# One split instruction per engine over a whole weight chunk, in a two-block transformer kernel

## The chip, the cores and the metric

The kernel runs on one core of one Trainium2 chip. The metric is the device time in microseconds (us) of one execution; the time before is the median of three runs. Five engines take part: TensorE (PE, with its weight loads shown apart as PEld), VectorE (DVE), ScalarE (ACT), GpSimd (POOL) and SyncE (SP), which here only issues DMAs. Each engine works off its own instructions strictly in the order in which the program gives them, and waits on semaphores of the others.

## What is computed

Two transformer stacks run one after the other over 256 tokens of width 1024, each two layers deep, all in float32. Every layer is a mixer and a gated feed-forward network, each behind an RMS norm. Cut to the parts that matter here:

```python
for l in range(2):                       # first block
    h = rms_norm(x, norm1_g[l]); proj = h @ w_in[l]          # 1024 x 3584
    ret = chunk_retention(...); sb = stick_breaking(...)     # 4 heads each
    x = x + concat([ret, sb]) @ w_out[l]
    h = rms_norm(x, norm2_g[l])
    x = x + (silu(h @ w_gate[l]) * (h @ w_up[l])) @ w_down[l]   # D_FF 2816
for l in range(2):                       # second block
    h = rms_norm(x, g_mix[l]); proj = h @ w_in_2[l]
    merged = sum over 3 branches of gate * (branch @ w_p)    # latent, dilated and neighbourhood attention
    x = x + merged @ w_o[l]
    h = rms_norm(x, g_ffn[l])
    x = x + (silu(h @ w1[l]) * (h @ w3[l])) @ w2[l]
return rms_norm(x, g_final)
```

## The kernel before

All weights lie in one array in memory, cut on the host into 502 chunks in the order of their use. A chunk is 128 partitions by 1024 columns of float32 (512 KB); 32 of them have 768 columns. Each chunk is loaded by one DMA into a tile `raw` (4 buffers), and is then split into a pair `hi`, `lo` (6 buffers each): ScalarE writes `hi`, the value rounded to the matmul's type, and VectorE writes `lo = raw - hi`. The products are made of three terms, `hi*hi`, `hi*lo` and `lo*hi`: `mm3` (lines 264 to 266) as three matmuls, `mmw` as two, one of 512 columns for `hi` against both parts of the activations (line 324) and one of 256 columns for `lo` (line 325).

The user of a chunk calls `chunk()`, which first asks for the splits of the next four chunks and for the loads of three more, and then hands out its own pair. So a chunk is normally split five uses ahead. A buffer of `hi` or `lo` comes free when the last matmul on it has run.

The split of a chunk is done today in pieces of `CUT = 512` columns: `hi` of the first half, `lo` of the first half, `hi` of the second half, `lo` of the second half. A matmul waits only for the pieces that it reads.

The order of the instructions on each engine is not written out by hand. A scheduler walks through a modelled execution, and gives each engine, when it is free in that model, the ready instruction of the highest priority. Priority is the order in which the program text asks for things, except in a block marked `high_priority` (`URGENT`), which is put ahead: the sums into the residual `x` and the norm that follows (`add`, lines 527 and 528, `norm_pair`, lines 452 and 453). An instruction that has begun isn't interrupted. On the chip the order is then fixed, and the times are not those of the model.

What else runs on ScalarE and VectorE, and so stands in the same two queues: `second` (line 366) copies one half of a product out of the accumulator bank, `whole` (line 371) adds the other half to it, both before the bank can be used again; in the attention parts `softmax_bank` (lines 850 to 861), `p_T` (line 867, the copy `pT` of transposed probabilities) and `finish`; at the start of a layer part the norm's `rsqrt` (line 402 on VectorE, then a power on GpSimd, line 403) and `row_bcast` (line 557, `diag`), which feeds two small matmuls.

At the end of `mixer2`, and at the beginning of each feed-forward network, `wide4` uses four chunks at once, column tile by column tile, and ends all four at nearly the same time.

Of the kernel before, what the change touches and what calls it, by code (L numbers as in the profile page):

```python
# [201 lines left out]
class Net:  # L202
# [16 lines left out]


    RAW, HI, LO = 4, 6, 6
    CUT = 512

    def fetch(self, upto):
        nc = self.nc
# [9 lines left out]
    def split(self, upto):  # L235
        nc = self.nc
        while self.next_split < min(upto, len(self.sizes)):
# [5 lines left out]
            lo = self.wp.tile([128, CW], F32R, tag="lo", bufs=self.LO, name="lo")  # L243
            for c in range(0, n, self.CUT):
                c = slice(c, min(n, c + self.CUT))
                nc.scalar.copy(out=hi[:, c], in_=raw[:, c])  # L246
# [889 lines left out]
```

## Time and profile before

| | |
|---|---|
| median of 3 runs | 1593.51 us (1593.07 to 1596.3) |
| the profiled execution | 1597.04 us, its span 1595.3 us |
| granted TensorE clock, mean over the span | 0.996 |
| busy: PE, PEld, DVE, ACT, POOL | 98%, 85%, 69%, 55%, 7% |
| memory read | 266.78 MB |

The span goes from the first to the last instruction; the 1.74 us by which the execution is longer lie around it. Busy times are unions of the instructions' records. Matmuls are pipelined and their ends are modelled, so PE's 98% says that it seldom stood still, and not that it was at its peak.

### The profile page before, as it was taken

Reading aid. Unit: us, or ns where it says so; the run is one execution under the profiler, and the core shown is the slowest. Engines: PE = TensorE matmul, PEld = TensorE weight load, DVE = VectorE, ACT = ScalarE, POOL = GpSimd, SP = SyncE. Lnnn points to the kernel's source line nnn. Section 1 sums busy time; section 2 is a strip of 40 time slices with the busy share of each in tenths; the row PEclk is TensorE's granted clock in tenths of the full one; section 3 lists DMA queues with packets and bytes.
Section 4 is the critical chain, followed back from the end, with each engine's and each line's share of the span. In section 5 each row is a group of like instructions: output and inputs, shape, how many; then the busy total and the mean of one; then the engine's idle time right before and its main releaser. Section 6 shows DMA issues by size and latency. Waiting matters only on the chain.

```text
span 1595.3 us, 23916 instructions
## 1 busy us (share of the span) xinstructions
PE 1568.5 (98%) x8908; PEld 1353.4 (85%) x8908; DVE 1106.1 (69%) x1957; ACT 872.5 (55%) x1687; POOL 117.8 (7%) x117
## 2 busy tenths in 40 slices
PE   9999999999999999999999999999999999999997
PEld 6888888888988888898888888888898888888886
DVE  7876777767777767775656677766775656677763
ACT  6555655555555555455544565555455544565552
POOL 2001000100110003100001110001000001110001
PEclk9999999999999999999999999999999999999998
DMA  7554655654455566533544465556433544465561
GB/s 255 178 157 161 202 190 183 193 176 140 158 175 196 180 187 230 177 106 106 185 139 159 136 207 185 181 181 223 161 107 109 186 136 159 143 200 189 178 185 55
DMA packets 78629, 269.39 MB, mean 169 GB/s; under 512 B 8625, under 2 KB 12849, under 8 KB 78385
## 3 DMA queue, kind: packets, MB, share of 16 engines
q1 hardware_dynamic: 78224, 267.34, 51.5%
q8 instruction: 70, 1.15, 0.3%
q10 hardware_dynamic: 288, 0.52, 0.1%
q14 instruction: 47, 0.38, 0.1%
HBM read 266.78 MB, written 1.05 MB: 168 GB/s over the span
## 4 chain that ended last, share of the span: by engine, by line
PE 94%; DVE 3%; issue 1%; ACT 1%; POOL 1%; DMA 0%; DVEq 0%; ACTq 0%
PE mm L324 36%; PE mm L325 18%; PE mm L266 9%; PE mm L265 9%; PE mm L264 9%; PE sc L269 4%; PE ov L269 3%; PE pt L416 2%; DVE lo L247 1%; PE pt L269 1%; ACT hi L246 1%; PE sc L265 0%; PE sc L266 0%; PE sc L264 0%; DVE xT L453 0%
## 5 line engine op out<-in xcount | busy, mean ns | idle before, releaser
L247 DVE TENSOR_TENSOR lo<-raw,hi 128x512 fp32r<-128x512 f32 x1004 | 669.8, 695 | 358.1 <-ACT hi L246 354.9
L246 ACT CAST hi<-raw 128x512 fp32r<-128x512 f32 x1004 | 581.3, 613 | 540.2 <-PE mm L324 204.5
L324 PE MATMUL mm<-xT,hi 128*128 128x512 f32 x1664 | 585.0, 396 | 5.2 <-DVE t L371 3.4
L325 PE MATMUL mm<-xT,lo 128*128 128x256 f32 x1664 | 466.6, 281 | 0.0
L324 PEld LDWEIGHTS mm<-xT,hi 128*128 128x128 f32 x1664 | 312.1, 188 | 79.2 <-DVE t L371 3.7
L325 PEld LDWEIGHTS mm<-xT,lo 128*128 128x128 f32 x1664 | 314.4, 189 | 0.3
L324 PE MATMUL mm<-hT,hi 128*128 128x512 f32 x704 | 246.6, 395 | 0.6 <-DVE t L371 0.6
L265 PE MATMUL mm<-lo,xT 128*128 128x512 f32 (+1 forms) x544 | 213.8, 393 | 1.7 <-DVE lo L247 1.7
L264 PE MATMUL mm<-hi,xT 128*128 128x512 f32 (+1 forms) x544 | 213.2, 392 | 1.1 <-ACT hi L246 1.1
L266 PE MATMUL mm<-hi,xT 128*128 128x512 f32 (+1 forms) x544 | 213.5, 392 | 0.0
L325 PE MATMUL mm<-hT,lo 128*128 128x256 f32 x704 | 197.4, 280 | 0.0
L324 PEld LDWEIGHTS mm<-hT,hi 128*128 128x128 f32 x704 | 131.9, 187 | 31.4 <-DVE t L371 0.7
L325 PEld LDWEIGHTS mm<-hT,lo 128*128 128x128 f32 x704 | 133.0, 189 | 0.0
L265 PEld LDWEIGHTS mm<-lo,xT 128*128 128x128 f32 x544 | 102.8, 189 | 21.3 <-DVE lo L247 2.9
L264 PEld LDWEIGHTS mm<-hi,xT 128*128 128x128 f32 x544 | 102.8, 189 | 20.0 <-ACT hi L246 1.6
L266 PEld LDWEIGHTS mm<-hi,xT 128*128 128x128 f32 x544 | 102.8, 189 | 18.1
L366 ACT COPY part<-mm 128x512 f32<-128x512 f32 x129 | 74.6, 578 | 10.1 <-PE mm L325 10.1
L472 POOL TENSOR_TENSOR acc<-acc,sq 128x256 f32<-128x256 f32 x58 | 60.9, 1053 | 169.0 <-ACT sq L463 166.3
L469 POOL TENSOR_TENSOR acc<-sq 128x256 f32<-128x256 f32 x10 | 15.0, 1507 | 690.7 <-ACT sq L463 690.7
L867 DVE COPY pT<-pt 128x512 f32<-128x512 f32 x48 | 33.1, 691 | 26.2 <-PE pt L416 26.0
L371 DVE TENSOR_TENSOR t<-mm,part 128x512 f32<-128x512 f32 (+1 forms) x61 | 41.3, 676 | 12.3 <-ACT part L366 12.3
L861 ACT ACTIVATE p<-p,nm 128x256 f32<-128x256 f32 (+1 forms) x48 | 27.5, 573 | 38.4 <-DVE nm L858 38.3
(220 smaller groups left out, 1740.3 us busy)
## 6 DMA issues: line engine op xcount, KB each, us to landing
raw<-w SPq DMA_DIRECT2D x470, 512.0 KB, 3.4
raw<-w SPq DMA_DIRECT2D x32, 384.0 KB, 3.0
bias<-bias SPq DMA_DIRECT2D x16, 256.0 KB, 3.2
c<-c SPq DMA_DIRECT2D x1, 1088.0 KB, 8.1
x<-x SPq DMA_DIRECT2D x4, 256.0 KB, 5.8
c<-c SPq DMA_DIRECT2D x1, 768.0 KB, 8.0
out<-y SPq DMA_DIRECT2D x2, 256.0 KB, 2.6
out<-y ACTq DMA_DIRECT2D x2, 256.0 KB, 3.2
```

The lines of the kernel that those rows point to most:

```text
L246: nc.scalar.copy(out=hi[:, c], in_=raw[:, c])
L247: nc.vector.tensor_tensor(out=lo[:, c], in0=raw[:, c], in1=hi[:, c].bitcast(F32), op=ALU.subtract)
L264: mm(out, l.hi, r.hi, start=start, stop=False, skip_group_check=True)
L265: mm(out, l.hi, r.lo, start=False, stop=False, skip_group_check=True)
L266: mm(out, l.lo, r.hi, start=False, stop=stop, skip_group_check=True)
L269: self.nc.tensor.matmul(out, l, r, start=start, stop=stop, skip_group_check=True)
L324: mm(flat(out), w.hi, flat(x.both[:, k, :, :]), start=start, stop=False, skip_group_check=True)
L325: mm(out[:, 0, :], w.lo, x.hi[:, k, :], start=False, stop=stop, skip_group_check=True)
L366: self.nc.scalar.copy(out=t, in_=b[:, :, 1, :])
L371: self.nc.vector.tensor_tensor(out=out, in0=b[:, :, 0, :], in1=self.second(b), op=ALU.add)
L472: nc.gpsimd.tensor_tensor(out=acc, in0=acc, in1=t, op=ALU.add)
L867: nc.vector.tensor_copy(out=t, in_=b)
```

## The change

The width of a piece of the split goes from 512 to 1024 columns, a whole chunk. The loop in `split()` then runs once for every chunk: one `hi` on ScalarE over all columns, and one `lo` on VectorE that waits for it. For the 32 chunks of 768 columns, which had a piece of 512 and one of 256, it is one piece of 768. Loads, buffers, the matmuls and all else stay as they are in the program text; the scheduler plans anew with the longer pieces.

```diff
     RAW, HI, LO = 4, 6, 6
-    CUT = 512
+    CUT = 1024
...
             for c in range(0, n, self.CUT):
                 c = slice(c, min(n, c + self.CUT))
                 nc.scalar.copy(out=hi[:, c], in_=raw[:, c])
                 nc.vector.tensor_tensor(out=lo[:, c], in0=raw[:, c], in1=hi[:, c].bitcast(F32), op=ALU.subtract)
```

## Rows read from the trace of the kernel before

**Rows 1.** The page: busy us, share of the span, instructions, by engine.

```profile
PE 1568.5 (98%) x8908; PEld 1353.4 (85%) x8908; DVE 1106.1 (69%) x1957; ACT 872.5 (55%) x1687; POOL 117.8 (7%) x117
```

**Rows 2.** The waits of TensorE: us in total, times, longest us.

```profile
PE pt L269 <- DVE diag L557: 4.0, 4, 1.6
PE mm L324 <- DVE t L371: 4.0, 5, 0.9
PE mm L324 <- DVE x L527: 3.6, 4, 0.9
...
PE mm L265 <- DVE lo L247: 1.7, 3, 0.8
...
PEld ov L269 <- DVE pT L867: 7.5, 20, 0.8
```

**Rows 3.** The waits of the split itself, same columns.

```profile
DVE lo L247 <- ACT hi L246: 354.9, 363, 6.5
...
ACT hi L246 <- PE mm L324: 204.5, 149, 6.6
```

**Rows 4.** Groups by line and shape: busy us, mean ns | idle before.

```profile
L247 DVE TENSOR_TENSOR lo<-raw,hi 128x512 fp32r<-128x512 f32 x972 | 657.4, 704 | 358.1 <-ACT hi L246 354.9
...
L246 ACT CAST hi<-raw 128x512 fp32r<-128x512 f32 x972 | 569.5, 619 | 540.2 <-PE mm L324 204.5 <-issue 157.1 <-PE mm L266 111.9
...
L247 DVE TENSOR_TENSOR lo<-raw,hi 128x256 fp32r<-128x256 f32 x32 | 13.3, 417 | 0.0
L246 ACT CAST hi<-raw 128x256 fp32r<-128x256 f32 x32 | 13.0, 405 | 0.0
```

**Rows 5.** The page's DMA issues: count, KB each, median us to landing.

```profile
raw<-w SPq DMA_DIRECT2D x470, 512.0 KB, 3.4
```

**Rows 6.** Timeline in a feed-forward network: start us, us, what.

```profile
249.85 0.39 PE L324 MATMUL mm<-xT,hi 128*128 128x512 f32 x1
...
250.19 0.39 PE L324 MATMUL mm<-xT,hi 128*128 128x512 f32 x1
...
251.01 1.14 ACT L246 CAST hi<-raw 128x512 fp32r<-128x512 f32 x2 [1.36 <-issue]
...
251.66 1.29 DVE L247 TENSOR_TENSOR lo<-raw,hi 128x512 fp32r<-128x512 f32 x2 [1.18 <-ACT hi L246]
```

**Rows 7.** Timeline of the start, VectorE, then TensorE.

```profile
18.82 3.70 DVE L247 TENSOR_TENSOR lo<-raw,hi 128x512 fp32r<-128x512 f32 x6
...
19.57 0.50 PE L265 MATMUL mm<-lo,xT 128*128 128x512 f32 x1 [0.78 <-DVE lo L247]
```

**Rows 8.** Timeline at the end of the first mixer2, ScalarE, VectorE, TensorE.

```profile
900.57 0.62 ACT L246 CAST hi<-raw 128x512 fp32r<-128x512 f32 x1 [6.56 <-PE mm L324]
901.10 0.58 ACT L366 COPY part<-mm 128x512 f32<-128x512 f32 x1
...
901.22 0.69 DVE L247 TENSOR_TENSOR lo<-raw,hi 128x512 fp32r<-128x512 f32 x1 [6.22 <-ACT hi L246]
901.83 0.69 DVE L527 TENSOR_TENSOR x<-mm,x 128x512 f32<-128x512 f32 x1
...
902.57 0.50 PE L324 MATMUL mm<-qk,hi 128*128 128x512 f32 x1 [0.88 <-DVE x L527]
```

**Rows 9.** Timeline of the norm before the first mixer2, VectorE, GpSimd, TensorE.

```profile
637.32 0.69 DVE L247 TENSOR_TENSOR lo<-raw,hi 128x512 fp32r<-128x512 f32 x1
637.93 0.16 DVE L402 TENSOR_SCALAR rs<-rf 128x2 f32<-128x2 f32 x1
638.00 0.68 DVE L247 TENSOR_TENSOR lo<-raw,hi 128x512 fp32r<-128x512 f32 x1
...
636.22 0.71 POOL L403 TENSOR_TENSOR rf<-rs,mh 128x2 f32<-128x2 f32 x1 [2.44 <-DVE rs L402]
...
638.16 1.07 POOL L403 TENSOR_TENSOR rf<-rs,mh 128x2 f32<-128x2 f32 x1 [0.96 <-DVE rs L402]
...
639.97 0.68 PE L269 MATMUL pt<-diag,c 128*128 128x128 f32 x4 [1.64 <-DVE diag L557]
```

## The prediction

> **What bounds the kernel now.** I read the page's busy times first: TensorE is busy 98% of the span, VectorE 69%, ScalarE 55% [rows 1]. Then the list of waits, TensorE's own: its largest entries are 1 to 8 us in total out of 1595.3, so the kernel is bound by the matmul stream, and a change to the other two engines can only act through these few waits [rows 2]. The reader is to see there that the split itself stops TensorE three times, for 1.7 us together; the other entries are sums and copies that stand in the same two queues as the split.
>
> Next, what the split waits for: ScalarE waits 204.5 us for TensorE to let go of buffers, VectorE 354.9 us for ScalarE [rows 3]. So the split runs ahead until all six buffers are full, and its pace is set by TensorE. Last, a feed-forward network's timeline: a pair of matmuls takes 0.34 us (249.85 to 250.19), the eight pairs of a chunk 2.7 us; in that time the split asks 1.14 us of ScalarE and 1.29 us of VectorE [rows 6]. A chunk is split five uses ahead, by estimate 5 x 2.7 = 13.5 us before it is read.
>
> **The change part by part.**
>
> *Shorter work.* A piece of 1024 columns isn't in the trace. By the groups of 256 and 512 columns [rows 4], one on ScalarE costs 405 + 3 x (619 - 405) = 1047 ns, against 1.14 us for two in a row: 0.09 us saved per chunk. On VectorE the same line gives 417 + 3 x (704 - 417) = 1278 ns; with the undisturbed 0.69 us instead of the mean it gives 417 + 3 x 273 = 1236. I take 1.25, which saves 0.04 us against the 1.29 of the pair. Over the 470 full chunks [rows 5] that is some 42 us less of ScalarE and 19 us less of VectorE (the bounds on VectorE: 470 x 0.01 = 5 and 470 x 0.05 = 24). None of it is on the path: the cover is the matmul stream, behind which each engine stands idle hundreds of us [rows 4]. I cost it at nothing. Were the cover gone, a chunk would cost 1.25 us of VectorE instead of 2.7 us of TensorE, so there is no danger from throughput either.
>
> *Later first half.* A matmul on columns 0 to 511 now waits for all 1024: `hi` comes 1.05 - 0.62 = 0.43 us later, `lo` 1.25 - 0.69 = 0.56 us after it has begun. With 13.5 us of lead that is hidden in the steady stretches. It isn't hidden at the start, where TensorE takes the pieces as they come: VectorE runs six in a row from 18.82, the first of them ends at 19.51, and the waiting matmul begins at 19.57 [rows 7]. With whole pieces that first one ends at 20.07; the three or four splits ahead of it give back 0.04 each. The start loses 0.4 us (bounds 0.2 and 0.6).
>
> *Longer blocks in an in-order queue.* This is what decides. Where the scheduler puts a split in front of an instruction on which TensorE waits, that one now stands behind 1.25 us of VectorE or 1.05 us of ScalarE, not 0.69 or 0.62. Where it used to slip an urgent instruction between two halves, it has to choose one side. Behind the late instruction queue, on VectorE, the sums that free the accumulator banks, and on ScalarE the copies `part` that do so with them. Stage by stage:
>
> The end of `mixer2`. There are four such waits for line 527, 3.6 us at the matmuls [rows 2]. In the one shown, `hi` begins at 900.57, half of `lo` at 901.22, the sum for which TensorE waits at 901.83, and the matmul at 902.57 [rows 8]. A whole `hi` ends at 901.62. If the sum now goes first, the bank waits for `part` instead, which moves from 901.10 to some 901.55 and ends 0.58 later, at 902.13: TensorE would start about 0.35 us sooner. If the whole `lo` goes first, it ends at 902.87 and the sum at 903.55, some 1.0 us later than today. I hold the first for about twice as likely, because in the model too `lo` must wait for the longer `hi`, and the sum has the higher priority: (2 x -0.35 + 1.0) / 3 = +0.1 each, +0.4 for four (bounds -1.4 and +4.0).
>
> The start of a feed-forward network. Five waits for `t` of line 371, 4.0 us [rows 2]. A whole split ahead of it in place of a half costs 0.56; one that isn't there costs nothing. No row excludes either; a quarter of the cases, as splits fill 669 of 1595 us of VectorE and part of those stretches has none ready, gives 5 x 0.14 = +0.7 us (bounds 0 and +2.8).
>
> The norm before the first `mixer2`. `rs` runs at 637.93, between the two halves that begin at 637.32 and 638.00; the power on GpSimd takes 1.07 us beside the second half and took 0.71 before; TensorE waits 1.64 us for what hangs on it [rows 9]. With one whole `lo` in front, `rs` begins at 638.57, 0.64 later, and the power is back at 0.71: +0.3. With `lo` behind it, `rs` begins some 0.5 sooner. I take +0.3, since nothing but `lo` is ready at 637.32 (bounds -0.5 and +0.6).
>
> Attention. TensorE waits 20 times for a `pT`, 7.5 us together [rows 2]. If such a copy meets VectorE at random, it waits for the rest of a split: busy share times half a length, 0.42 x 0.345 = 0.14 us now (670 us of 1595), 0.39 x 0.625 = 0.24 then (625 us of 1595). That is +0.10 each, 2.0 us for twenty; the planner fills the gaps with other matmuls, so I take half, +1.0 (bounds 0 and 4.8, the whole of the 0.24).
>
> Sum: 0.4 + 0.4 + 0.7 + 0.3 + 1.0 = +2.8 us. The profiled execution is 1597.04, 1.74 us more than its span, and 3.5 us above the median of 1593.51; that is the spread of the runs, not another kernel. So 1599.8 on its own scale, and 1596.3 on that of the median. The bounds add to -1.7 and +12.8, that is 1591.8 and 1606.3.
>
> **The rivals.** *Faster.* At the block ends the urgent sums overtake, and the splits get out of the way of the softmax chain. It gives 4 x -0.35 at line 527, -0.5 at the norm, and, if the twenty copies meet 0.10 us less each rather than more, -2.0; with the start's +0.4 that is -3.5, so 1590.0. The lower busy shares speak for it, the longer residual of every split against it. It decides if at all four ends of `mixer2` line 527 stands ahead of `lo`.
>
> *Slower, by blocking.* The planner is greedy: it starts a split when nothing else is ready, and the urgent instruction comes a moment later. With the upper bound at line 527 (4.0), all of the feed-forward starts (2.8), 2.0 in attention and 0.7 at start and norm it is +9.5, 1603.0; half of it is 1598.3. For it speaks that in rows 8 and 9 a half already stands just ahead of the instruction that TensorE waits for. It decides from three of the nine block waits on.
>
> *GpSimd held out.* The power took 1.07 us instead of 0.71 beside a half of `lo` [rows 9]. If a whole `lo` holds it for up to 0.56 us more, at the four `diag` waits [rows 2] and once for each of the eight layer parts' norms, it adds up to 12 x 0.56 = 6.7; with the likeliest sum and a third of this, 1598.5. Against it: most of GpSimd's work is far from the path, as it is busy 7% [rows 1]. The Trainium skill ("SBUF — State Buffer", section "Who interferes with whom") states that VectorE with two SBUF inputs and a reading GpSimd instruction exclude each other for a whole instruction, and that the second fully blocks. By that rule a longer `lo` is a longer hold, and this rival would be the rule wherever a power meets a split; the trace agrees in kind, with 0.36 us added where 0.52 us of the split (638.16 to 638.68) remained, so less than the rule gives.
>
> **How the numbers follow.** Two tenths of a per cent, 3.2 us, is about what a measurement of this kernel can tell from no change. The forecast, a sum that stays within that, has 0.47; slower by blocking 0.28; GpSimd held out 0.13; faster 0.12. So faster 0.12, same 0.47, slower 0.41. The predicted time is 1596.3. The range leaves out the last parts of both ends: below 1591.5 some 0.08 (most of the faster rival), above 1603.0 some 0.10 (blocking at all places at once). It needs no more, as throughput has no part in it.
>
> **What would show it.** In the profile after: 502 instructions on each of lines 246 and 247, means near 1.05 and 1.25 us, busy sums about 530 and 625 us; line 324 and 325 with the same means and counts; TensorE's wait for `lo` at the start longer by 0.4 us; the order around 901 us (line 527 ahead of or behind `lo`); the wait for `pT` some tenths of a us larger per softmax. The prediction is wrong if a piece of 1024 columns costs more than the line through 256 and 512 gives, if the planner's new order moves matmuls between stages and so opens waits where none are now, or if the waits at the block ends shrink together.

## The result, and the profile after

| | before | after |
|---|---|---|
| first comparison, median | 1593.56 us (4 runs, 1593.07 to 1596.3) | 1612.03 us (4 runs, 1609.86 to 1615.57) |
| ratio to before | | 1.0116, interval 1.0096 to 1.0136 |
| the same two kernels, measured again later | 1599.93 us (17 runs, 1593.3 to 1603.6) | 1611.45 us (6 runs, 1604.17 to 1618.87) |
| ratio to before | | 1.0072, interval 1.0046 to 1.0098 |
| profiled execution | 1597.04, span 1595.3, clock 0.996 | 1610.6, span 1608.7, clock 0.994 |

The change makes the kernel slower, by 18 us in the first comparison and 11.5 in the second, where +2.8 was forecast. Both medians after lie above the range of 1591.5 to 1603.0, and so does the fastest single run, 1604.17. The two ratios don't agree well. That is a finding of its own, taken up under *cadence* below: the kernel before, with nothing changed, had medians between 1593.56 and 1599.93.

First the page's busy line after, to lay beside [rows 1]:

```profile
PE 1571.3 (98%) x8908; PEld 1354.4 (84%) x8908; DVE 1071.4 (67%) x1455; ACT 826.3 (51%) x1185; POOL 120.8 (8%) x117
```

VectorE is 35 us less busy and ScalarE 46, with 502 instructions fewer on each, and the span is 13.4 us longer. The work that was saved bought no time. Next the groups by line and shape, for [rows 4]:

```profile
L247 DVE TENSOR_TENSOR lo<-raw,hi 128x1024 fp32r<-128x1024 f32 x470 | 579.4, 1235 | 377.4 <-ACT hi L246 376.5
```

```profile
L246 ACT CAST hi<-raw 128x1024 fp32r<-128x1024 f32 x470 | 492.2, 1051 | 563.1 <-PE mm L324 330.9 <-PE mm L266 141.0 <-issue 45.1
```

A whole piece takes 1235 and 1051 ns; the forecast had 1.25 and 1.05 us. The price was right, and both engines still idle hundreds of us. So the loss is looked for in the waits of TensorE, which answer to [rows 2]:

```profile
PE mm L324 <- DVE x L527: 7.5, 4, 1.9
PE mm L324 <- DVE t L371: 6.8, 5, 1.6
PE pt L269 <- DVE diag L557: 4.1, 5, 1.4
...
PE mm L265 <- DVE lo L247: 0.8, 1, 0.8
...
PEld ov L269 <- DVE pT L867: 8.2, 24, 0.8
```

The two places at which a four-chunk product ends have grown, `x` from 3.6 to 7.5 us and `t` from 4.0 to 6.8, while `diag` and `pT` have hardly moved and `lo` has fallen. The timeline at the end of the first `mixer2`, in the place of [rows 8], shows how (start, us, engine, what):

```profile
913.36 1.05 ACT L246 CAST hi<-raw 128x1024 fp32r<-128x1024 f32 x1 [6.22 <-PE mm L324]
...
914.21 0.27 PE L325 MATMUL mm<-qk,lo 128*128 128x256 f32 x1
914.32 1.06 ACT L366 COPY part<-mm 128x512 f32<-128x512 f32 x2
914.45 1.22 DVE L247 TENSOR_TENSOR lo<-raw,hi 128x1024 fp32r<-128x1024 f32 x1 [6.38 <-ACT hi L246]
...
915.59 1.28 DVE L527 TENSOR_TENSOR x<-mm,x 128x512 f32<-128x512 f32 x2
...
916.33 0.50 PE L324 MATMUL mm<-qk,hi 128*128 128x512 f32 x1 [1.85 <-DVE x L527]
```

The reader is to follow four steps. The product uses four chunks in turn, and the first of them comes free 0.85 us before the last matmul (914.21), which lets a `hi` start at 913.36. ScalarE can begin `part` only behind it, at 914.32. VectorE, idle for 6.38 us, next has the whole `lo` of that same chunk, from 914.45, and behind it the urgent sum of line 527, at 915.59. TensorE starts again at 916.33, after 1.85 us instead of 0.88. The order is the planner's and not a matter of what is ready: the sum's bank takes the products of the first two of the four chunks, which were done two pairs of matmuls before the end. Before, the order was the same with a half: `lo` from 901.22, the sum at 901.83.

The start of the first feed-forward network has the same shape, but there `t` needs `part` as well, and so the `lo` was ready first:

```profile
143.65 1.05 ACT L246 CAST hi<-raw 128x1024 fp32r<-128x1024 f32 x1 [5.75 <-PE mm L324]
...
144.72 1.22 DVE L247 TENSOR_TENSOR lo<-raw,hi 128x1024 fp32r<-128x1024 f32 x1 [5.63 <-ACT hi L246]
...
145.94 0.68 DVE L371 TENSOR_TENSOR t<-mm,part 128x512 f32<-128x512 f32 x1
...
146.67 0.49 PE L324 MATMUL mm<-xT,hi 128*128 128x512 f32 x1 [1.57 <-DVE t L371]
...
148.14 0.63 PE L324 MATMUL mm<-xT,hi 128*128 128x512 f32 x1
...
148.78 0.63 PE L324 MATMUL mm<-xT,hi 128*128 128x512 f32 x1
```

The last two lines show something else: after the stall a pair of matmuls takes 0.64 us, not the 0.34 of [rows 6]. The table by stretches says why (us; PE busy and matmuls; then the granted clock, the DMA share, GB/s):

```profile
146.00:148.00 2.00, 1.22 (x6) 0.91 0.51 147
148.00:150.00 2.00, 2.00 (x8) 0.50 0.28 115
150.00:152.00 2.00, 2.00 (x11) 0.74 0.78 262
152.00:154.00 2.00, 2.00 (x13) 1.00 0.79 254
```

From 148 us the granted clock is 0.50, that is 1.2 instead of 2.4 GHz, and it is back at 152. In these 4 us 19 matmuls start instead of 26. From the last pair ahead of the stall to the first matmul on `hT` it is 117.56 us by the starts of line 324; in the second network, with the same stall, the same cadence (below) and no fall of the clock, it is 116.02: the fall costs 1.5 us. In the kernel before the granted clock stays at 1.00 through the same place, with its stall of 0.86 us.

### The profile page after: what moved, and what is told of

Same layout as the page of the kernel before. It is cut to its first block, busy times and chain, and to the rows that moved or that the text cites. A ratio compares the mean times of both kernels' runs of the same rounds, so it can differ in the third digit from the quotient of the medians.

```text
span 1608.7 us, 22929 instructions
## 1 busy us (share of the span) xinstructions
PE 1571.3 (98%) x8908; PEld 1354.4 (84%) x8908; DVE 1071.4 (67%) x1455; ACT 826.3 (51%) x1185; POOL 120.8 (8%) x117
## 3 DMA queue, kind: packets, MB, share of 16 engines
HBM read 266.78 MB, written 1.05 MB: 166 GB/s over the span
## 4 chain that ended last, share of the span: by engine, by line
PE 91%; DVE 3%; ACT 2%; issue 2%; POOL 1%; DMA 0%; DVEq 0%; ACTq 0%
PE mm L324 35%; PE mm L325 18%; PE mm L265 9%; PE mm L264 9%; PE mm L266 9%; PE sc L269 4%; PE ov L269 3%; PE pt L416 2%; DVE lo L247 1%; ACT hi L246 1%; PE pt L269 1%; POOL mg L949 0%; PE sc L265 0%; PE sc L266 0%; POOL hrs L403 0%
## 5 line engine op out<-in xcount | busy, mean ns | idle before, releaser
L247 DVE TENSOR_TENSOR lo<-raw,hi 128x1024 fp32r<-128x1024 f32 (+1 forms) x502 | 610.6, 1218 | 396.8 <-ACT hi L246 395.8
L246 ACT CAST hi<-raw 128x1024 fp32r<-128x1024 f32 (+1 forms) x502 | 518.9, 1038 | 597.6 <-PE mm L324 364.0
L324 PE MATMUL mm<-qk,hi 128*128 128x512 f32 x128 | 45.0, 397 | 3.7 <-DVE x L527 3.7
```

Of the source, the lines that this page charges most:

```text
L247: nc.vector.tensor_tensor(out=lo[:, c], in0=raw[:, c], in1=hi[:, c].bitcast(F32), op=ALU.subtract)
L324: mm(flat(out), w.hi, flat(x.both[:, k, :, :]), start=start, stop=False, skip_group_check=True)
```

## The experiments

Since the time of one kernel moves by steps of some 3.3 us from run to run (below), each is read first by its waits and by what its profiled execution says place by place, and only then by its ratio.

**One engine at a time.** Only `hi` whole, then only `lo` whole.

```diff
+            whole = slice(0, n)                                   # only hi whole
+            nc.scalar.copy(out=hi[:, whole], in_=raw[:, whole])
             for c in range(0, n, self.CUT):
                 c = slice(c, min(n, c + self.CUT))
-                nc.scalar.copy(out=hi[:, c], in_=raw[:, c])
```

```diff
-                nc.vector.tensor_tensor(out=lo[:, c], ...)        # only lo whole
+            whole = slice(0, n)
+            nc.vector.tensor_tensor(out=lo[:, whole], ...)
```

> Only the ScalarE piece is whole (1024 columns), the VectorE piece stays in halves. Theory 1, blocking at the block ends by the whole VectorE piece: what TensorE waits for at the ends is a VectorE sum, and this stands behind a half again, so most of the loss is gone: 1594 to 1600 us, waits for x of line 527 near 0.9 to 1.3 us each and for t of line 371 near 0.8 to 1.2. Rival, the ScalarE piece blocks the copies out of the banks: as slow as the change, 1606 to 1613. Rival, cadence (a pair of matmuls takes 347 or 353 ns in whole stretches, by accident of where the stream restarts): any time from 1590 to 1606, with stretches of the feed-forward networks at 353 ns where the time is long.

> Only the VectorE piece is whole, the ScalarE piece stays in halves. Theory 1: the whole VectorE piece stands ahead of the sums at the ends, so the loss is nearly that of the change: 1604 to 1613 us, waits for x of line 527 near 1.7 to 2.0 us each. Rival, ScalarE blocks: 1594 to 1599. Rival, cadence: no relation to which engine's piece is whole.

Only `hi` whole: 1608.52 us beside 1593.75 before, ratio 1.0092 (1.0063 to 1.012). Its waits of TensorE (a line added above shifts the numbers by one):

```profile
PE mm L325 <- DVE x L528: 5.4, 4, 1.4
PE mm L325 <- DVE t L372: 4.7, 5, 1.0
```

Only `lo` whole: 1605.83 us, ratio 1.0083 (1.0061 to 1.0106), with

```profile
PE mm L325 <- DVE x L528: 3.1, 4, 0.8
...
PE pt L671 <- DVE o L711: 2.7, 4, 0.7
PE mm L325 <- DVE t L372: 2.3, 5, 0.6
```

Each alone is slower. In the profiled executions three and two of the four feed-forward networks were slow (see *cadence*); less 3.3 us for each, the spans are 1597.0 and 1595.5, where the kernel before has 1588.7 by the same reckoning. A whole `hi` makes the ends of four-chunk products longer. A whole `lo` alone doesn't: there the planner lets the sum go first (at the end of the first `mixer2` the sum of line 528 runs at 909.42, the `lo` at 910.02), and both waits fall, to 3.1 and 2.3. What it costs is inside the attention parts: the output product of the first block's mixer goes from 25.32 to 26.25 us, twice, and the second block's first mixer, from its norm's first small matmul to the first product on `yT`, from 155.99 to 157.55 (all by the starts of matmuls); with only `hi` whole these are 25.14 and 156.35, and that kernel loses at other waits (`o` 2.6 us, 0.6 before). So the loss has two sources, the two pieces don't simply add up, and the ends need both pieces whole to reach 1.9 and 1.6 us.

**Which chunks.** Whole pieces everywhere but for the six chunks split around the end of a four-chunk product, and the reverse.

```diff
-            for c in range(0, n, self.CUT):
-                c = slice(c, min(n, c + self.CUT))
+            cut = 512 if i in self.near else 1024      # the reverse: 1024 if ..., else 512
+            for c in range(0, n, cut):
+                c = slice(c, min(n, c + cut))
...
     def wide4(self, xT, nk=NKT):
+        self.near |= set(range(self.next_use + 5, self.next_use + 11))
```

> Whole pieces everywhere, but halves for the six chunks that are split around the end of each use of four chunks at once (the end of mixer2, the start of a feed-forward network): 8 such places. Theory 1: the block-end waits go back to those of before (about 1.0 us at line 527, 0.9 at t), which returns 4 x 1.0 + 4 x 0.7 = 6.7 us and the clock drops behind the long waits; what stays is the loss inside the mixers, some 4 to 6 us: 1597 to 1602. Rival, the loss is spread over all whole pieces: 1608 or more. Rival, cadence: the feed-forward stretches decide, up to 3.3 us each.

> The complement: halves everywhere, whole pieces only for the six chunks around each of the 8 places. Theory 1: the block-end waits are those of the change (2.0 us at line 527, 1.6 at t), 6.7 us and the clock drops behind them: 1600 to 1606. Rival, spread over all pieces: within 2 us of before.

Halves near the ends: 1603.01 us (1595.87 to 1608.98), ratio 1.0057 (1.0035 to 1.008); `x` and `t` are back at 3.6 and 4.0 us. Whole pieces only near the ends: 1609.78 us, ratio 1.0105 (1.0079 to 1.0131), and

```profile
PE mm L326 <- DVE x L530: 7.4, 4, 1.9
PE mm L326 <- DVE t L374: 6.8, 5, 1.6
```

Those are the waits after the change (lines shifted by three), brought back by a small share of the chunks. This is the experiment that settles the places: the ends carry about half of the loss, the attention parts the other half. Taking 3.3 us off the span for each slow network (below) leaves 1588.7 us for before (1595.3 less two), 1594.0 for halves near the ends (none), 1594.9 for whole pieces near the ends (1608.1 less four), and 1600.6 after (1608.7 less two, less the 1.5 of the clock). So the parts are +5.3 and +6.2, together 11.5, and the change +11.9.

**The kernel before, once more, and quarters.**

> The kernel before, unchanged, for a second trace. Theory 3, cadence: in some feed-forward networks a pair of matmuls takes 346.7 ns all along, in others 353.3 ns, which is 3.3 us for a network; which it is falls out anew in every execution. Then the networks that are slow differ from the first trace (the third and fourth), and the time is near 1590.4 + 3.3 us for each slow one. Rival, the cadence belongs to the program: the third and the fourth are slow again and the time is 1597.

> Pieces of 256 columns everywhere. Theory 1, blocking: shorter blocks in front of the urgent instructions, waits at line 527 near 0.7 us and at t near 0.8, so 1 to 3 us less waiting than before, unless the four instructions per engine and chunk (by the rows 4 x 0.4 us on each) fill the queues: 1588 to 1597 us. Rival, what counts is the number of instructions: slower than before by 3 us or more. Cadence adds 0 to 13 us to any of it in steps of 3.3.

The kernel before again took 1593.82 us (one run) with the same waits; one network was slow, and 1592.0 less 3.3 is 1588.7 once more. With `CUT = 256` it is 1598.66 us beside 1596.92, ratio 1.0001 (0.999 to 1.0012); `x` 3.5 and `t` 4.0 us as with halves. Below a half, a finer piece frees the sums no sooner. The equal times are luck of the cadence: one network was slow in the profiled execution, and 1596.9 less 3.3 is 1593.6, or 4.9 us more than halves; its lowest run, 1595.19, fits that. Among the waits that grew are those in attention, `o` to 2.5 and `pT` to 9.3 us.

**Splits held back at the ends.** The next four splits wait for `part` and for the sum, with halves and with whole pieces, so that no split can stand in front of the sum.

```diff
+    def hold_splits(self):
+        self.gate = (self.part_ins, self.sum_ins)
+        self.held = set(range(self.next_split, self.next_split + 4))
...
+            first, second = self.gate if i in self.held else (None, None)
+                with self.tc.issue_after(first) if first else nullcontext():
                     nc.scalar.copy(out=hi[:, c], in_=raw[:, c])
+                with self.tc.issue_after(second) if second else nullcontext():
                     nc.vector.tensor_tensor(out=lo[:, c], ...)
```

> The kernel before, halves, with the four chunks whose splits come next after each use of four chunks at once held back behind the copies and sums that free the banks. Theory 1: the half in front of the sum at the four ends of mixer2 goes, 0.6 us each, and little changes at the feed-forward starts: 2 to 3 us less waiting than before. Rival, the sum isn't limited by the split in front of it but by the matmuls: same waits. Cadence adds 0 to 13 us in steps of 3.3.

> The changed kernel, whole pieces, with the same holding back. Theory 1: the waits at the ends fall from 2.0 to about 0.4 us (line 527) and from 1.6 to about 0.9 (t), 4 x 1.6 + 4 x 0.7 = 9 us less waiting than the change, so at most 3.5 us of waiting more than before, from the mixers. Rival, whole pieces cost wherever they stand: the time of the change. Cadence adds 0 to 13 us in steps of 3.3.

Halves: 1608.26 us, ratio 1.0062 (1.0043 to 1.0081). Whole: 1616.68 us, ratio 1.0105 (1.008 to 1.0129). With whole pieces the waits are (lines 246, 527 and 371, shifted)

```profile
PE mm L328 <- ACT hi L249: 4.1, 9, 1.1
PE mm L329 <- DVE lo L251: 3.6, 6, 0.7
PE mm L328 <- DVE x L536: 2.9, 4, 0.8
PE mm L328 <- DVE t L380: 2.4, 6, 0.6
```

The sums did go first, `x` and `t` fell below those of the kernel before, and the time rose all the same: TensorE now waits for `hi` and `lo`, which it never did at these places. That overturns my picture of a queue in which only the order is wrong. A product that works four chunks at once holds four of the six buffer pairs to its end, so only two splits can be ahead, and the next four-chunk product reads all four in its first four pairs, 1.4 us. At the ends the split and the sum are both on the path, and neither order of whole pieces that was tried serves both; halves, taken in turn with the sums, serve both best of what was tried.

**The buffers, not the order.** If that is so, a second four-chunk product that works its chunks one after the other should lose less, as buffers come free one by one.

```diff
-    def wide4(self, xT, nk=NKT):
+    def wide4(self, xT, nk=NKT, in_turn=False):
         outs = [self.quad() for _ in range(2)]
+        if in_turn:
+            for j in range(4):
+                self.wide1(outs[j // 2][:, j % 2], xT, nk)
+            return outs
...
-                for j, b in enumerate(self.wide4(mT)):
+                for j, b in enumerate(self.wide4(mT, in_turn=m > 0)):
```

> Whole pieces, but the second four-chunk product of each mixer2 works its four chunks one after the other. My theory: four chunks used at once leave only two of six buffer pairs for the splits ahead, and at the end three splits and the sums meet; in turn, the buffers come free one by one, so at the two ends that follow such a product the wait for x falls from 2.0 to about 1 us: x in total 7.5 to some 5.5, time 1 to 4 us below the changed kernel (1608 to 1611). Rival: what counts is only the planner's choice of lo before the sum, and the waits for x stay at 2.0 each, 7.5 in total.

> The same with halves, as in the kernel before. My theory: the wait for x falls by 0.5 us or more in two of its four places, from 3.6 in total to some 2.5, and the time is 0 to 1.5 us below the kernel before: the cleanest candidate for a version that beats both. Rival: the planner's choice alone counts; the wait for x stays at 3.6 and the time is the same within 0.1%.

> The changed kernel once more, unaltered. If the loss belongs to the planned order, TensorE's waits are those of the first trace within 0.2 us each (x of line 527 near 7.5, t of line 371 near 6.8), and the time stands 9 to 16 us above the kernel before, mostly +12.5 plus steps of some 3.3 us. If each network draws its cadence anew in every execution, other networks than the first and second show 353 ns a pair this time. Rival: the cadence belongs to the program, and the first and second network are slow again.

With whole pieces `x` fell by 2.9 us (lines 371 and 527 shifted by three):

```profile
PE mm L324 <- DVE t L374: 6.9, 5, 1.6
PE mm L324 <- DVE x L530: 4.6, 4, 1.9
```

and the end that follows the product in turn shows, in the timeline,

```profile
930.65 0.50 PE L324 MATMUL mm<-xT,hi 128*128 128x512 f32 x1 [0.45 <-DVE x L530]
```

0.45 us where two of four were 1.9. That is what the buffers would give, but the run doesn't single them out. In turn, the first accumulator bank (of two chunks) is complete half a product earlier: its sum runs at 923.40, and TensorE goes from the last matmul on `qk` (927.95) straight on into the network's products, to stop only for the second bank. The order is another too: that bank's sum, at 929.91, stands ahead of the whole `lo`, at 930.51. So whether the buffers held together are part of the cause stays open. The time shows no gain: 1612.83 us, ratio 1.0082 (1.0059 to 1.0106), beside 1611.45 for the changed kernel on the same chip. Its profiled execution fell to half clock after six stalls and had two slow networks; the changed kernel's second one after three, with no slow network. Without them that is 1614.3 - 9.0 - 6.6 = 1598.7 and 1605.8 - 4.5 = 1601.3, a gain of 2.6 us.

With halves, in turn, it is 1597.15 us (1593.46 to 1600.65), ratio 0.9982 (0.9966 to 0.9998). But the wait for `x` rose from 3.6 to 4.4 us, against what I expected. At the first end after a product in turn VectorE has three halves of `lo` ahead of the second bank's sum, and TensorE waits 1.33 us, so here too the sum stands behind the split:

```profile
916.49 2.97 DVE L247 TENSOR_TENSOR lo<-raw,hi 128x512 fp32r<-128x512 f32 x3
919.38 0.68 DVE L530 TENSOR_TENSOR x<-mm,x 128x512 f32<-128x512 f32 x1
```

Less its two slow networks the span is 1594.9 - 6.6 = 1588.3, 0.4 under before. So this is the kernel before within what can be told, and no version here beats it in earnest.

The changed kernel again had its waits to the tenth (`x` 7.5, `t` 6.8), and more stalls with a fall of the clock: three this time, at the start of the first network as before and at the two ends of the last `mixer2`, of which this is the second (columns as above):

```profile
1402.00:1404.00 2.00, 0.34 (x2) 1.00 0.02 6
1404.00:1406.00 2.00, 2.00 (x8) 0.50 0.70 256
1406.00:1408.00 2.00, 2.00 (x9) 0.65 0.28 63
```

**The cadence.** One tiny matmul, its result unused, at equal distances in the feed-forward networks of the kernel before.

```diff
                 else:
+                    with self.tc.issue_after(self.last_mm):
+                        self.mm(self.bank("ov")[:, :16], self.warm[:, :128], self.warm[:, :16])
                     G, U = self.wide2(xT), self.wide2(xT)
```

> The kernel before, with one tiny extra matmul of 16 columns (result unused) behind each group of products of a feed-forward network, ten times per network at equal distances. If a break in the even stream sets the cadence, stretches of 346.7 and 353.3 ns a pair follow one another inside one network, with the changes at the extra matmuls. Rival: the cadence is set at a network's start and holds to its end, so each network shows one of the two values throughout. Cost of the extra matmuls: 40 of some 0.1 us, 2 to 6 us in all.

It took 1600.43 us, one run. The timeline has the extra matmuls at

```profile
156.14 0.18 PE L269 MATMUL ov<-warm 128*128 128x16 bf16 x1
...
167.56 0.18 PE L269 MATMUL ov<-warm 128*128 128x16 bf16 x1
...
178.79 0.19 PE L269 MATMUL ov<-warm 128*128 128x16 bf16 x1
...
190.22 0.18 PE L269 MATMUL ov<-warm 128*128 128x16 bf16 x1
```

and line 324 between them, in the groups by shape of the first and the second of these stretches (mean ns last but one):

```profile
L324 PE MATMUL mm<-xT,hi 128*128 128x512 f32 x32 | 11.4, 401 | 0.0
```

```profile
L324 PE MATMUL mm<-xT,hi 128*128 128x512 f32 x32 | 11.2, 396 | 0.0
```

The same 32 pairs and one extra matmul take 11.42, then 11.23, then 11.43 us, and so on to the last extra matmul of the network: the cadence changes at each extra matmul, to and fro, by 0.19 / 32 = 6 ns a pair. A break in the stream of matmuls can switch it.

## Why the prediction was wrong

**Bound, throughput, prices: right.** TensorE stayed the bound; 1235 and 1051 ns stand against 1.25 and 1.05 us; the steady stretches hid the whole pieces. Halves near the ends show that: whole pieces in all other chunks cost nothing inside the networks, whose waits for `t` are the 4.0 us of before.

**The start: right in size, at another place.** It was put at +0.4 (0.2 to 0.6). The small matmul on `acc` that closes the first products comes at 22.53 instead of 22.22, +0.3. The longer wait for `lo` that was to show it isn't there (one wait of 0.8 us instead of three, 1.7). The later piece is the very first `hi`, for which the first product waits 0.47 us longer (before, then after):

```profile
7.00 0.49 PE L264 MATMUL mm<-hi,xT 128*128 128x512 f32 x1 [1.06 <-ACT hi L246]
```

```profile
7.47 0.62 PE L264 MATMUL mm<-hi,xT 128*128 128x512 f32 x1 [2.00 <-ACT hi L246]
```

The granted clock is at 0.50 until 14.5 us, before until 12.1, so the +0.3 holds that too, and that it meets the forecast is in part luck.

**The end of `mixer2`: the step that failed.** It was taken at +0.1 each, because the sum was held twice as likely to go first; measured are (7.5 - 3.6) / 4 = +0.97 each, the stated worst case "if the whole `lo` goes first". The argument was that in the planner's model too `lo` must wait for the longer `hi`, and that the sum has the higher priority. On the chip the sum's bank was indeed complete first, and still `lo` stands ahead. This could be read from [rows 8]: `part` begins at 901.10 and reads the same bank as the sum, so the sum could have run then, but VectorE waited for `hi` and took half of `lo` at 901.22. The order that the planner had chosen for a half was the best evidence for a whole piece, and the step went against it. Why its model has `lo` first no trace shows.

**The start of a network: mis-sized in the same way.** Taken at a quarter of 0.56 us, +0.14 at each of five waits; measured are +2.8 in all, which is the upper bound only by luck. The fifth wait lies at products on `hT` and stayed at 0.6 us; the four at the starts of networks went from some 0.85 to 1.56 us, +0.7 each, more than the bound for one. The bound counted the longer `lo` alone (0.56), but the `lo` also begins later, behind the longer `hi`. The chance that a split is ready at an end isn't VectorE's busy share: the end itself makes one ready, as the first of four chunks comes free.

**The lead of 13.5 us.** It was worked out for one chunk at a time and holds in the steady stretches. At the ends a four-chunk product holds four of the six pairs, so only two can be ahead; the held-back splits show it, in waits for `hi` and `lo` of 4.1 and 3.6 us.

**The norm before `mixer2`: wrong in sign, and small.** Taken at +0.3; the wait fell from 1.64 to 1.35 us, since `rs` now runs ahead of `lo` (the timeline after, for [rows 9]):

```profile
648.95 0.17 DVE L402 TENSOR_SCALAR rs<-rf 128x2 f32<-128x2 f32 x1
649.03 1.23 DVE L247 TENSOR_TENSOR lo<-raw,hi 128x1024 fp32r<-128x1024 f32 x1
649.20 1.61 POOL L403 TENSOR_TENSOR rf<-rs,mh 128x2 f32<-128x2 f32 x1 [0.47 <-DVE rs L402]
...
651.55 0.68 PE L269 MATMUL pt<-diag,c 128*128 128x128 f32 x4 [1.35 <-DVE diag L557]
```

**GpSimd held out: the mechanism is there, its price isn't.** The power takes 1.61 us beside a whole `lo`, 1.07 beside a half and 0.71 alone: 0.90 us more where 1.06 us of `lo` was left (649.20 to 650.26). The Trainium skill ("SBUF — State Buffer", section "SBUF: two separate sides") has the two exclude each other for a whole instruction; the trace agrees but for 0.16 us, as it did with halves (0.36 of 0.52). But most powers lie off the path: the `diag` waits went from 4.0 to 4.1 us, and this rival's 6.7 us never came.

**Attention: the wrong wait.** Taken at +1.0 (0 to 4.8) through `pT`, which rose by 0.7, from 7.5 to 8.2. The parts lost more, some 5 us by the kernel with halves near the ends, and in the stretches measured above it is a whole `lo` that does it. The loss is spread over many places of a few tenths of a us (`o` of line 710 went from 0.7 to 1.8 in total); which of them the planner's new order made, and which the longer holds, wasn't separated. The forecast named a new order that moves matmuls and opens new waits as a sign of its being wrong. Inside these parts that is so: taken in order, TensorE's 8908 matmuls differ by their tiles at 1042 places between before and after, and matmuls wait 1.6 us in all for `va` of line 990, `x` of line 530 and `ra` of line 619, which stand for no matmul in the list of before.

**The sum.** Measured are 3.9 + 2.8 at the ends and starts, about 5 in attention, 0.3 at the start and -0.3 at the norm, 11.7 in all, in agreement with the +11.9 of the two profiled executions (the 5 is what another run had left over, and its cause is open). The rival "slower, by blocking", with 0.28, had the mechanism, and its +9.5 is 2 us short, in attention. It was the forecast that should have been made, since [rows 8] has a half `lo` already ahead of a sum that could run. Two things stood in no sum: the clock after the longer stalls, 1.5 us each, and the cadence. With one such fall the 11.9 become the 13.4 us between the two spans. That the clock and the cadence make the rest of the 18 us of the first comparison fits their sizes, but isn't shown, as its other runs left no trace.

## What to carry to other kernels

Before making pieces of background work longer, look at the places where several buffers and an accumulator bank come free together: there the background work becomes ready beside the urgent one, and where the trace of before has it ahead, expect it to stay ahead; cost it at the full longer hold, of both pieces where one waits for the other, and not at the engine's busy share. A lead counted in chunks holds only while the chunks are used one at a time. And when a kernel's time moves in steps between runs, find the step before reading differences of its size: here it was as large as the effect looked for.

## What the runs showed of the hardware

**Two cadences.** The pair of lines 324 and 325 runs at one of two rates for a whole feed-forward network, at the same granted clock of 1.00. Groups by shape in the kernel before, first 470 to 550 us, then 950 to 1030 us:

```profile
L324 PE MATMUL mm<-xT,hi 128*128 128x512 f32 x232 | 80.5, 391 | 0.0
```

```profile
L324 PE MATMUL mm<-xT,hi 128*128 128x512 f32 x228 | 80.6, 399 | 0.0
```

232 and 228 pairs in the same 80 us. By the starts of the matmuls a pair takes 346.7 or 353.3 ns; a network has 528 pairs, and its two products, from the last pair ahead of the stall on, take 113.2 and 60.7 us or 115.3 and 61.8, 3.3 us apart. Which networks are slow differs between executions of one program: the third and fourth in the kernel before, only the first in its second profile; the first and second in the kernel after, none in its second profile. So runs of one kernel fall on steps: 17 of the kernel before at 1593.3 and 1593.4, 1596.7, 1599.1 to 1600.3 (ten runs) and 1602.5 to 1603.6. The extra matmuls show that a break can flip it. What decides it at a network's start, and why its long-run share differs between chips or sessions, stays open.

**The clock after a stall.** Stalls of 1.6 to 1.9 us at the ends were followed in some executions, not in all, by 3 to 4 us at a granted clock near 0.5, at 1.5 us apiece: at one of eight such places in the first profile after, at three of eight in the second, at all six with the product in turn, and at none of eight with whole pieces only near the ends. With stalls of 1.4 us and less at the same places (kernel before, only `hi` whole, only `lo` whole) the mean clock of every run was 0.996 or more; after the change it was 0.991 to 0.996. A wait that is 1 us longer can thus cost 2.5. The length of a single stall doesn't settle it, though. In the kernel with whole pieces held back, whose runs had 0.986 to 0.995, no stall at the four ends of `mixer2` was above 0.8 us, and in its profile the clock fell at two of them. At the first of the two, TensorE had stalled for 0.8 us for `x` and for 0.3 and 0.4 us for `hi` when the clock fell, during a fourth stall of 0.7 us for `lo` (columns as above):

```profile
926.00:928.00 2.00, 1.15 (x4) 1.00 0.00 0
928.00:930.00 2.00, 1.45 (x5) 0.58 0.23 53
```
